# A hybrid encoder on one core: work moved between VectorE, GpSimd and two stages of the kernel, and three loads and adds put elsewhere

## The chip, the cores and the metric

The kernel runs on one core of a Trainium2 chip. The metric is the device time of one execution in microseconds. The profile is one further execution taken by the hardware profiler. Engines are named as the profile names them: PE (TensorE, with PEld for its weight loads), DVE (VectorE), ACT (ScalarE), POOL (GpSimd), and SP, whose queue issues most of the DMAs.

## The reference

An encoder trunk with two layers works on `x` (1024 positions by 1024 channels, float32). Layer 0 mixes positions by attention, layer 1 by a gated MLP over chunks of 128 positions (gMLP); each is followed by a dense MLP with 4096 hidden channels. Every sub-layer has its input normalized and modulated by vectors that come from the condition `c`, and its output gated by one. Cut to what matters here:

```python
for i in range(DEPTH):                       # 2 layers
    mod = silu(c) @ ada_w[i] + ada_b[i]      # six vectors of 1024 for each layer
    sh1, sc1, g1, sh2, sc2, g2 = split(mod, 6)
    h = modulate(rmsnorm(x, norm1_g[i]), sh1, sc1)
    y = gqa_attention(h, ...) if i == 0 else chunked_gmlp(h, ...)
    x = x + g1 * y
    h = modulate(rmsnorm(x, norm2_g[i]), sh2, sc2)
    x = x + g2 * (square(relu(h @ w_in)) @ w_out)

# in gqa_attention: o = softmax(q k^T / 8) v over 16 heads;  return o @ w_o
# in chunked_gmlp:  u, v = split(gelu(h @ w_in + b_in));  v = layernorm(v), mixed within chunks
#                   return (u * v) @ w_out
```

## The kernel before, in words

`x` is held transposed, as 16 tiles of 128 channels by 512 positions: `x[hf][k]`, `hf` the half of the positions and `k` the channel block. Products are made in float32 accuracy from three matmuls of 128x512: each operand is split in a rounded part `hi` (a cast on ACT) and the rest `lo` (a subtraction on DVE); L294 and L295 in `split` do this for activations, L407 and L408 for weights. Large products use one step of a Winograd (Strassen) scheme: seven products of half-size blocks, called "1" to "7", in place of eight. This needs sums of blocks ahead of the matmuls, which are called *forms*, and sums of results behind them. A *unit* below is one product of one pair of blocks: 12 matmuls.

The stages follow one another: q, k and v (0 to 196 us), attention in 64 units (about 190 to 586), the product with `w_o` ("WO", to 674), MLP0's products with `w_in` (to 997, 112 units), MLP0 Out (to 1319, 112 units), gMLP's v (to 1560), gMLP's u (to 1841), gMLP Out (to 2090, 84 units), MLP1's products (to 2406) and MLP1 Out. A table of constants at the end of the file sets when things are done; a scheduler then orders the instructions of each engine, and each engine takes its own in that order. Instructions wrapped in `pin` stay where they are written.

*The vectors from `c`.* Each of the twelve vectors of 1024 is eight columns. Some are made early. `Slabs` makes four groups of eight in attention: a step loads a 128x1024 slab of `ada_w` (L173, on SP, into one of four `w` buffers, three steps ahead), multiplies it on POOL (L186 or L188) and adds it on POOL (L189); at a group's end PE does eight matmuls of one column (L198, tile `am`). A step is taken in 5 of 8 units from unit 10 on. `Halves` makes 24 more columns during MLP0's products, one per step, a step every `MX` = 3 units: two loads of 256 KB (L1214, into two of 16 `x` buffers) and two multiply-sums on DVE (L1226).

*WO's preparation.* At attention's unit `WO_AT` = 53 `load_sel` loads the two halves of a small matrix `sel` (L778, SP) and casts each on DVE (L779); the following units use it in `wo_prep`. The weights of WO come through the same `w` buffers (load L107, cast on ACT L110).

*The heads.* At the start of each MLP and of gMLP the second half's norm is made: squares are summed on DVE (L240), PE sums them over channels (L249, tile `ss`, in unit `HB` = 1 of the MLPs), the root is made, PE spreads it (`rb`, L260), and `forms_b` (from L324) makes the forms of that half: the products with `rb` (`norm_h`, L300), two sums on DVE (L342, L343), a split, and two sums on POOL (L345, L346). For gMLP two of the eight `norm_h` are on POOL (`NB`). Beside them `winograd`'s `prep` makes the weights' sums (L400, L401, L404, L406): on POOL for the first `IG` = 30 units, on DVE after. In `wino_v` (gMLP's v) the sums of block "6" are L1390 to L1392, all on POOL but one.

*The Out stages.* `Out.run` takes the products in the order 1, 2, 6, 4, 7 and then, in a tail, 5 and 3. Results of "6" and "7" that must be added to `x[1]` are kept in tiles and added in the tail's first eight units, `6` at even and `7` at odd units (`add`, L1116: `x<-t` on DVE).

## Time and profile before

| | us |
|---|---|
| median of 3 runs | 2731.7 |
| lowest and highest of these | 2727.88 and 2733.51 |
| the profiled execution | 2724.75 |
| its span on the page | 2723.0 |

The page counts 37313 instructions in the span. PE is busy for 96% of it, DVE 82%, ACT 53%, POOL 39%; the DMA queues move 435 MB. How to read the lines below: a group shows line, engine, operation, the tiles `out<-in` by the program's names, and then busy time or the mean of one in ns; a timeline row shows the start, the duration in us, the engine and the line, and in square brackets how long the engine had idled before it, with what released it; a window shows the length, then for each engine the busy time with the count of instructions, then the granted TensorE clock (1.00 is full), the share of the DMA engines and GB/s.

### The profile page before, as it was taken

Reading aid. Unit: us, or ns where it says so; the run is one execution under the profiler, and the core shown is the slowest. Engines: PE = TensorE matmul, PEld = TensorE weight load, DVE = VectorE, ACT = ScalarE, POOL = GpSimd, SP = SyncE. Lnnn points to the kernel's source line nnn. Section 1 sums busy time; section 2 is a strip of 40 time slices with the busy share of each in tenths; the row PEclk is TensorE's granted clock in tenths of the full one; section 3 lists DMA queues with packets and bytes.
Section 4 is the critical chain, followed back from the end, with each engine's and each line's share of the span. In section 5 each row is a group of like instructions: output and inputs, shape, how many; then the busy total and the mean of one; then the engine's idle time right before and its main releaser. Section 6 shows DMA issues by size and latency. Waiting matters only on the chain. (4 is left out here: it accounts for less than half of the span.)

```text
span 2723.0 us, 37313 instructions
## 1 busy us (share of the span) xinstructions
PE 2627.7 (96%) x12804; PEld 2182.2 (80%) x12804; DVE 2232.0 (82%) x3127; ACT 1450.9 (53%) x2618; POOL 1061.1 (39%) x725
## 2 busy tenths in 40 slices
PE   7999999899899999999999999999999999999999
PEld 5778999787688878877788888887878788878877
DVE  7978888688889889897897767787988887789993
ACT  4559999764654555436443355444446555455432
POOL 1437677644300025451633265556632200035520
PEclk9999999999899999999999999999999999999999
DMA  7120111235386688633334345558641364477461
GB/s 282 62 70 24 50 64 60 80 124 170 97 287 227 217 297 313 211 118 130 114 124 132 114 161 182 182 200 291 223 128 59 128 206 143 166 266 276 143 208 67
DMA packets 207601, 435.39 MB, mean 160 GB/s; under 512 B 22897, under 2 KB 35313, under 8 KB 207410
## 3 DMA queue, kind: packets, MB, share of 16 engines
q1 hardware_dynamic: 180530, 395.24, 43.1%
q10 hardware_dynamic: 26880, 37.76, 3.8%
q8 instruction: 101, 1.65, 0.2%
q14 instruction: 90, 0.74, 0.1%
HBM read 310.23 MB, written 122.68 MB: 159 GB/s over the span
## 5 line engine op out<-in xcount | busy, mean ns | idle before, releaser
L1101 PE MATMUL out<-t,s 128*128 128x512 f32 x1232 | 484.4, 393 | 11.7 <-DVE t L295 11.7
L1102 PE MATMUL out<-t,s 128*128 128x512 f32 x1232 | 482.9, 393 | 7.8 <-DVE s L1085 7.8
L1100 PE MATMUL out<-t,s 128*128 128x512 f32 x1232 | 483.9, 393 | 5.9 <-ACT t L294 5.9
L422 PE MATMUL w<-t,s 128*128 128x512 f32 x1168 | 460.3, 395 | 0.5 <-ACT t L294 0.5
L424 PE MATMUL w<-t,s 128*128 128x512 f32 x1168 | 455.2, 390 | 0.9 <-DVE s L408 0.9
L423 PE MATMUL w<-t,s 128*128 128x512 f32 x1168 | 455.2, 390 | 0.0
L295 DVE TENSOR_TENSOR t<-t,t 128x512 fp32r<-128x512 f32 x408 | 379.6, 944 | 44.7 <-ACT t L294 31.9
L294 ACT CAST t<-t 128x512 fp32r<-128x512 f32 x408 | 244.7, 616 | 174.7 <-DMA t<-hf 57.6
L407 ACT CAST s<-w 128x512 fp32r<-128x512 f32 x292 | 174.7, 618 | 239.2 <-PE w L424 135.2
L1101 PEld LDWEIGHTS out<-t,s 128*128 128x128 f32 x1232 | 233.2, 189 | 66.5 <-DVE t L295 17.4
L1102 PEld LDWEIGHTS out<-t,s 128*128 128x128 f32 x1232 | 233.5, 190 | 59.2 <-DVE s L1085 11.2
L1100 PEld LDWEIGHTS out<-t,s 128*128 128x128 f32 x1232 | 233.1, 189 | 56.9 <-ACT t L294 8.2
L408 DVE TENSOR_TENSOR s<-w,s 128x512 fp32r<-128x512 f32 x292 | 225.0, 778 | 58.9 <-ACT s L407 58.1
L1071 POOL TENSOR_TENSOR w<-w,t 128x512 f32<-128x512 f32 x32 | 50.7, 1590 | 547.8 <-DMA hf<-t 251.7
L422 PEld LDWEIGHTS w<-t,s 128*128 128x128 f32 x1168 | 219.7, 188 | 49.6 <-issue 3.8
L424 PEld LDWEIGHTS w<-t,s 128*128 128x128 f32 x1168 | 219.7, 188 | 47.2 <-DVE s L408 1.3
L423 PEld LDWEIGHTS w<-t,s 128*128 128x128 f32 x1168 | 219.7, 188 | 45.7 <-issue 1.0
L1085 DVE TENSOR_TENSOR s<-t,s 128x512 fp32r<-128x512 f32 x240 | 211.6, 883 | 53.9 <-ACT s L1084 51.8
L1084 ACT CAST s<-t 128x512 fp32r<-128x512 f32 x240 | 147.5, 620 | 169.9 <-PE out L1102 98.4
L878 DVE TENSOR_TENSOR t<-t,t 128x512 fp32r<-128x512 f32 x256 | 164.3, 683 | 23.8 <-ACT t L872 23.4
L855 DVE TENSOR_REDUCE mx<-s 128x1 f32<-128x1024 f32 x128 | 156.5, 1223 | 31.4 <-PE s L852 30.4
L869 PE MATMUL t<-ident,c 128*128 128x128 f32 x1024 | 150.7, 275 | 16.4 <-DVE t L878 11.9
(252 smaller groups left out, 5405.6 us busy)
## 6 DMA issues: line engine op xcount, KB each, us to landing
t<-hf SPq DMA_DIRECT2D x320, 256.0 KB, 3.8
hf<-c SPq DMA_DIRECT2D x156, 256.0 KB, 3.3
w<-in_wi_dram SPq DMA_DIRECT2D x64, 512.0 KB, 4.5
hf<-c ACTq DMA_DIRECT2D x96, 256.0 KB, 2.1
w<-in_adan_dram SPq DMA_DIRECT2D x32, 512.0 KB, 3.3
t<-in_wm_dram SPq DMA_DIRECT2D x64, 256.0 KB, 4.8
wf<-w SPq DMA_DIRECT2D x64, 256.0 KB, 2.9
t<-wf SPq DMA_DIRECT2D x64, 256.0 KB, 3.3
```

Of the source, the lines that this page charges most:

```text
L294: S.copy(hi, src)
L295: (eng or V).tensor_tensor(lo, src, f32(hi), ALU.subtract)
L407: S.copy(hi, src)
L408: V.tensor_tensor(lo, src, f32(hi), ALU.subtract)
L422: T.matmul(ps, hi[:, a], th, start=kt == 0, stop=False)
L423: T.matmul(ps, hi[:, a], tl, start=False, stop=False)
L424: T.matmul(ps, lo[:, a], th, start=False, stop=kt == 3)
L878: pin(V.tensor_tensor(lo, pt, f32(hi), ALU.subtract))
L1085: V.tensor_tensor(lo, src, f32(hi), ALU.subtract)
L1100: T.matmul(ps, hi[:, a], th, start=begin and kt == 0, stop=False)
L1101: T.matmul(ps, hi[:, a], tl, start=False, stop=False)
L1102: T.matmul(ps, lo[:, a], th, start=False, stop=end and kt == 3)
```

## The change

It has six edits. `Slabs` loses the group (1, 2), and these eight columns are made by `Halves`, which now has 32 and takes a step every 2 units. `load_sel` is called at unit 47, and the casts (`copy_sel`, on ACT, pinned) stay at 53. The sums L345 and L346 of `forms_b`, the two `norm_h` of `NB`, and the early sums of `prep` go from POOL to DVE; in `wino_v` the first pair's three sums of "6" go to DVE, and those of the other two pairs stay (one on DVE, two on POOL). `HB` is 2 for MLP0 and stays 1 for MLP1. The adds of the "6" results into `x[1]` start at half of the tail (`tail` is 32 units in the MLPs, 24 in gMLP).

```diff
--- before.py
+++ after.py
@@ -156,7 +156,7 @@
                                1.0, ng[:, layer, which, k : k + 1], ALU.add, ALU.mult)
 
     pending = [(0, j, k) for j in (2, 4, 3) for k in range(KT)]
-    late = [(0, 5, k) for k in range(KT)] + [(1, j, k) for j in (3, 5) for k in range(KT)]
+    late = [(0, 5, k) for k in range(KT)] + [(1, j, k) for j in (2, 3, 5) for k in range(KT)]
 
 
 
@@ -202,7 +202,7 @@
                 V.scalar_tensor_tensor(amod[:, layer, which], mod[:, layer, j], 1.0, ng[:, layer, which],
                                        ALU.add, ALU.mult)
 
-    slabs = Slabs([(1, 1), (1, 0), (1, 2), (1, 4)])
+    slabs = Slabs([(1, 1), (1, 0), (1, 4)])
 
     def mods(n, tag="w"):
         for _ in range(min(n, len(pending))):
@@ -321,7 +321,7 @@
             f["todo"].pop(0)()
             n -= 1
 
-    def forms_b(f, xt, layer, which, rb, order, nb=()):
+    def forms_b(f, xt, layer, which, rb, order):
 
         raw = f.pop("raw")
         src = {q: [None] * 4 for q in "345678"}
@@ -329,8 +329,8 @@
         b12, b22, t3 = src["5"], src["3"], src["7"]
 
         def h(kt):
-            b12[kt] = norm_h(xt[kt], layer, which, kt, rb, G if kt in nb else V)
-            b22[kt] = norm_h(xt[kt + 4], layer, which, kt + 4, rb, G if kt + 4 in nb else V)
+            b12[kt] = norm_h(xt[kt], layer, which, kt, rb, V)
+            b22[kt] = norm_h(xt[kt + 4], layer, which, kt + 4, rb, V)
 
         def forms(kt):
             if kt == 0:
@@ -342,8 +342,8 @@
             V.tensor_tensor(t3[kt], b22[kt], b12[kt], ALU.subtract)
             V.tensor_tensor(t2, b11, t3[kt], ALU.add)
             f[("6", kt)] = split(t2)
-            G.tensor_tensor(b12[kt], b12[kt], b11, ALU.subtract)
-            G.tensor_tensor(b21, b21, t2, ALU.subtract)
+            V.tensor_tensor(b12[kt], b12[kt], b11, ALU.subtract)
+            V.tensor_tensor(b21, b21, t2, ALU.subtract)
 
         def later(q):
             for kt in range(4):
@@ -394,16 +394,15 @@
             hi, lo = w_[:, :512], w_[:, 512:]
             sf[(q, p)] = hi, lo
             src = half(p, {"1": "11", "2": "12", "6": "11", "5": "21", "4": "22", "7": "22", "3": "12"}[q])
-            e = G if i < IG else V
             if q == "6":
                 a11, a21, a22 = (half(p, c) for c in ("11", "21", "22"))
-                e.tensor_tensor(a21, a21, a22, ALU.add)
-                e.tensor_tensor(a11, a21, a11, ALU.subtract)
+                V.tensor_tensor(a21, a21, a22, ALU.add)
+                V.tensor_tensor(a11, a21, a11, ALU.subtract)
             elif q == "4":
                 a12 = half(p, "12")
-                e.tensor_tensor(a12, a12, half(p, "11"), ALU.subtract)
+                V.tensor_tensor(a12, a12, half(p, "11"), ALU.subtract)
             elif q == "7":
-                e.tensor_tensor(src, src, half(p, "11"), ALU.subtract)
+                V.tensor_tensor(src, src, half(p, "11"), ALU.subtract)
             S.copy(hi, src)
             V.tensor_tensor(lo, src, f32(hi), ALU.subtract)
             if q == "3":
@@ -774,10 +773,15 @@
 
     def load_sel():
         for i in range(2):
-            raw, s_ = slot(F32, (32, 512)), slot(F32R, (32, 512))
+            raw = slot(F32, (32, 512))
             nc.sync.dma_start(raw, t["sel"][:, i * 512 : (i + 1) * 512])
-            V.tensor_copy(s_, raw)
-            sel.append(s_)
+            sel.append(raw)
+
+    def copy_sel():
+        for i in range(2):
+            s_ = slot(F32R, (32, 512))
+            pin(S.copy(s_, sel[i]))
+            sel[i] = s_
 
     def wo_sums(hf):
         ri = small.tile([P, 4, NH], F32, tag="ri", name=nm("ri"), bufs=1)
@@ -957,9 +961,11 @@
                 if f == "m":
                     if i in deferred:
                         deferred.pop(i)()
+                    elif i == WO_AT - 6:
+                        load_sel()
                     elif WO_AT <= i < WO_AT + 10:
                         if i == WO_AT:
-                            load_sel()
+                            copy_sel()
                         elif i == WO_AT + 1:
                             wo_sums(0)
                         else:
@@ -1104,8 +1110,11 @@
                     for kt in range(4):
                         del self.f[(b, q, kt)]
                 j = i - self.n + self.tail
-                if 0 <= j < 8:
-                    self.add(1, j % 2, j // 2, self.acc[("67"[j % 2], j // 2)])
+                late = j - self.tail // 2
+                if 0 < j < 8 and j % 2:
+                    self.add(1, 1, j // 2, self.acc[("7", j // 2)])
+                elif 0 <= late < 8 and late % 2 == 0:
+                    self.add(1, 0, late // 2, self.acc[("6", late // 2)])
                 if end:
                     self.take(i, b, q, p, ps, done)
                 if hook:
@@ -1260,7 +1269,7 @@
         def at(i):
             more(f, RW, None)
             if halves:
-                h = i - HB - 12
+                h = i - 13
                 if 0 <= h < 2 * KT:
                     spill(h // KT, (h % KT,))
                 elif h == 2 * KT:
@@ -1271,11 +1280,11 @@
                     halves.load()
                 elif h > 2 * KT + 6 and h % MX == 0:
                     halves.step()
-            if i == HB:
+            if i == HB[layer]:
                 rest.append(norm_ss(sqs[0], bank_y))
-            elif i == HB + 1:
+            elif i == HB[layer] + 1:
                 rest[:] = forms_b(f, x[1], layer, 1, norm_rb(rest[0], bank_y, True), "5473")
-            elif i > HB and rest:
+            elif i > HB[layer] and rest:
                 rest.pop(0)()
             if stores and i % 7 > 0 and i % 7 != 6:
                 stores.pop(0)()
@@ -1387,9 +1396,10 @@
             src = {"1": a11, "2": a12, "7": a11, "5": a21, "4": a22, "3": a12}.get(q)
             if q == "6":
                 src = xslot()
-                G.tensor_tensor(a11, a11, a21, ALU.subtract)
-                (V if p else G).tensor_tensor(src, a22, a11, ALU.subtract)
-                G.tensor_tensor(a12, a12, src, ALU.subtract)
+                e = G if p else V
+                e.tensor_tensor(a11, a11, a21, ALU.subtract)
+                V.tensor_tensor(src, a22, a11, ALU.subtract)
+                e.tensor_tensor(a12, a12, src, ALU.subtract)
             elif q == "5":
                 G.tensor_tensor(a21, a21, a22, ALU.add)
             S.copy(hi, src)
@@ -1501,7 +1511,7 @@
                 spill(0)
                 rest.append(norm_ss(sqB, bank_y))
             elif i == HBV + 2:
-                rest[:] = forms_b(f, x[1], 1, 0, norm_rb(rest[0], bank_y), "7543", NB)
+                rest[:] = forms_b(f, x[1], 1, 0, norm_rb(rest[0], bank_y), "7543")
             elif i > HBV + 2 and rest and (i <= HBV + 6 or i % 2):
                 rest.pop(0)()
                 if len(rest) == 4:
@@ -1647,15 +1657,14 @@
 LO = 3
 TG = ((0, 0), (1, 0), (1, 1), (0, 1))
 CUT = 8
-MX = 3
+MX = 2
 LW = 5
-IG = 30
 SW = 3
 WA = 6
 LW2 = 2
 HK = 3
 LK = 4
-HB = 1
+HB = (2, 1)
 HBV = 1
 PRE = 2
 WO_AT = 53
@@ -1663,7 +1672,6 @@
 RQ = 3
 RW = 2
 NA = (7,)
-NB = (3, 7)
 WOM = (0, 2, 1, 1, 2, 3, 4, 1)
 PREP = ((0, 1, 2), (3, 4, 5), (6, 7))
 QM = (0, 0, 0, 1, 0, 1, 2, 2, 2, 0)
```

On SP, at the end of attention, the loads stood in this order before (`in_adan` are the slabs, `in_sel` the two halves of `sel`, `in_xT` tiles of `x`):

```order
L173 DMA w_5806<-in_adan_dram 128x1024
L173 DMA w_5892<-in_adan_dram 128x1024
L473 DMA x_6939<-in_xT_dram 128x512
L473 DMA x_6941<-in_xT_dram 128x512
L173 DMA w_6060<-in_adan_dram 128x1024
L473 DMA x_6943<-in_xT_dram 128x512
L473 DMA x_6945<-in_xT_dram 128x512
L173 DMA w_6158<-in_adan_dram 128x1024
L778 DMA t_6052<-in_sel_dram 32x512
L173 DMA w_6421<-in_adan_dram 128x1024
L778 DMA t_6056<-in_sel_dram 32x512
```

and now, from behind the last slab on (`in_ada` is a column of the vectors, `in_wo` the first weight of WO):

```order
L777 DMA t_5549<-in_sel_dram 32x512
L777 DMA t_5551<-in_sel_dram 32x512
L472 DMA x_6897<-in_xT_dram 128x512
L472 DMA x_6899<-in_xT_dram 128x512
L472 DMA x_6901<-in_xT_dram 128x512
L472 DMA x_6903<-in_xT_dram 128x512
L472 DMA x_6905<-in_xT_dram 128x512
L472 DMA x_6907<-in_xT_dram 128x512
L472 DMA x_6909<-in_xT_dram 128x512
L472 DMA x_6911<-in_xT_dram 128x512
L139 DMA w_6970<-in_ada_dram 128x1024
L107 DMA w_6975<-in_wo_dram 128x1024
```

Both `sel` loads stand together ahead of the tiles of `x`, and no slab stands behind or between them.

On DVE, at MLP0's head, behind the row that uses `rb` first (`t` are forms, `x` the second half's tiles):

```order
L300 TENSOR_TENSOR t_8092<-x_7117,rb_8070 128x512
L300 TENSOR_TENSOR t_8095<-x_7125,rb_8070 128x512
L300 TENSOR_TENSOR t_8098<-x_7119,rb_8070 128x512
L300 TENSOR_TENSOR t_8101<-x_7127,rb_8070 128x512
L342 TENSOR_TENSOR t_8104<-t_8095,t_8092 128x512
L343 TENSOR_TENSOR t_8105<-t_7641,t_8104 128x512
L295 TENSOR_TENSOR t_8109<-t_8105,t_8108 128x512
L300 TENSOR_TENSOR t_8134<-x_7121,rb_8070 128x512
L300 TENSOR_TENSOR t_8137<-x_7129,rb_8070 128x512
L342 TENSOR_TENSOR t_8140<-t_8101,t_8098 128x512
L343 TENSOR_TENSOR t_8141<-t_7644,t_8140 128x512
L295 TENSOR_TENSOR t_8145<-t_8141,t_8144 128x512
```

and now:

```order
L300 TENSOR_TENSOR t_8070<-x_7075,rb_8048 128x512
L300 TENSOR_TENSOR t_8073<-x_7083,rb_8048 128x512
L300 TENSOR_TENSOR t_8076<-x_7077,rb_8048 128x512
L300 TENSOR_TENSOR t_8079<-x_7085,rb_8048 128x512
L342 TENSOR_TENSOR t_8082<-t_8073,t_8070 128x512
L343 TENSOR_TENSOR t_8083<-t_7599,t_8082 128x512
L345 TENSOR_TENSOR t_8070<-t_8070,t_7599 128x512
L346 TENSOR_TENSOR t_7658<-t_7658,t_8083 128x512
L295 TENSOR_TENSOR t_8087<-t_8083,t_8086 128x512
L295 TENSOR_TENSOR t_8095<-t_7993,t_8094 128x512
L300 TENSOR_TENSOR t_8113<-x_7079,rb_8048 128x512
L300 TENSOR_TENSOR t_8116<-x_7087,rb_8048 128x512
```

L345 and L346, on POOL before, stand behind L343 in each of the four steps, ahead of the split's subtraction L295.

On DVE, in the tail of MLP0 Out (L1085 and L295 are the subtractions that PE's operands wait for; `x<-t` are the adds of kept results, `x<-out` those from PSUM), the scheduler had put the four adds of "6" (`x_11014` to `x_11020`) among the splits:

```order
L295 TENSOR_TENSOR t_12736<-t_12659,t_12735 128x512
L1116 SCALAR_TENSOR_TENSOR x_11016<-t_11103,mod,x_11016 128x512
L295 TENSOR_TENSOR t_12760<-t_12684,t_12759 128x512
L1151 TENSOR_TENSOR t_11163<-out_12694,t_11163 128x512
L1085 TENSOR_TENSOR s_12740<-t_12290,s_12740 128x512
L295 TENSOR_TENSOR t_12784<-t_12709,t_12783 128x512
L1116 SCALAR_TENSOR_TENSOR x_11018<-t_11129,mod,x_11018 128x512
L1116 SCALAR_TENSOR_TENSOR x_10907<-out_12719,mod,x_10907 128x512
L1085 TENSOR_TENSOR s_12764<-t_12320,s_12764 128x512
L295 TENSOR_TENSOR t_12808<-t_12733,t_12807 128x512
L1116 SCALAR_TENSOR_TENSOR x_11020<-t_11163,mod,x_11020 128x512
L1116 SCALAR_TENSOR_TENSOR x_10909<-out_12743,mod,x_10909 128x512
```

The same place now (line numbers are 6 to 9 higher):

```order
L295 TENSOR_TENSOR t_12721<-t_12643,t_12720 128x512
L1091 TENSOR_TENSOR s_12700<-t_12354,s_12700 128x512
L295 TENSOR_TENSOR t_12745<-t_12668,t_12744 128x512
L1160 TENSOR_TENSOR t_11138<-out_12678,t_11138 128x512
L1091 TENSOR_TENSOR s_12725<-t_12383,s_12725 128x512
L295 TENSOR_TENSOR t_12769<-t_12693,t_12768 128x512
L295 TENSOR_TENSOR t_12793<-t_12718,t_12792 128x512
L295 TENSOR_TENSOR t_12817<-t_12742,t_12816 128x512
L1160 TENSOR_TENSOR t_11172<-out_12703,t_11172 128x512
L1091 TENSOR_TENSOR s_12749<-t_12299,s_12749 128x512
L1125 SCALAR_TENSOR_TENSOR x_10916<-out_12728,mod,x_10916 128x512
```

and three of the adds of "6" (`x_11025` to `x_11029` from a `t`) stand here, some 90 rows on; the first, `x_11023`, stands 21 rows ahead of them:

```order
L295 TENSOR_TENSOR t_13369<-t_13302,t_13368 128x512
L1091 TENSOR_TENSOR s_13405<-t_13274,s_13405 128x512
L1091 TENSOR_TENSOR s_13436<-t_13309,s_13436 128x512
L1125 SCALAR_TENSOR_TENSOR x_11025<-t_11112,mod,x_11025 128x512
L295 TENSOR_TENSOR t_13377<-t_13276,t_13376 128x512
L1091 TENSOR_TENSOR s_13461<-t_13337,s_13461 128x512
L1091 TENSOR_TENSOR s_13492<-t_13372,s_13492 128x512
L1125 SCALAR_TENSOR_TENSOR x_11027<-t_11138,mod,x_11027 128x512
L1125 SCALAR_TENSOR_TENSOR x_11029<-t_11172,mod,x_11029 128x512
```

In between are the adds of "7" and the start of the last blocks; the splits that stood around the adds have moved up by one or two rows.

## The prediction

> **What bounds the kernel now.** The page first: the span, and the share of each engine.

> ```profile
> span 2723.0 us, 37313 instructions
> PE 2627.7 (96%) x12804; PEld 2182.2 (80%) x12804; DVE 2232.0 (82%) x3127; ACT 1450.9 (53%) x2618; POOL 1061.1 (39%) x725
> ```

> PE is the bound, so a gain can come only from the 95 us in which it does nothing and from stretches where it runs slowly. The windows view finds those (length, then busy time and instructions of PE, PEld, DVE, ACT, POOL, then the granted clock).

> ```profile
> 480.00:600.00 120.00, 106.13 (x672) 92.10 (x671) 89.10 (x121) 83.72 (x161) 71.04 (x49) 0.94 0.29 94
> 673.00:742.00 69.00, 58.69 (x231) 45.62 (x230) 57.43 (x75) 43.07 (x79) 29.05 (x19) 0.90 0.23 73
> 742.00:1000.00 258.00, 258.00 (x1140) 213.64 (x1139) 222.37 (x412) 131.96 (x225) 5.24 (x4) 1.00 0.76 257
> 1195.00:1250.00 55.00, 50.06 (x212) 39.55 (x211) 49.53 (x63) 23.65 (x45) 20.22 (x13) 0.97 0.48 144
> 1319.00:1370.00 51.00, 43.95 (x182) 33.86 (x181) 47.59 (x56) 26.23 (x44) 38.27 (x26) 0.97 0.15 52
> 1990.00:2045.00 55.00, 49.16 (x200) 38.30 (x199) 48.90 (x63) 22.84 (x43) 18.89 (x12) 0.94 0.44 138
> 2090.00:2152.00 62.00, 57.38 (x237) 45.09 (x235) 50.94 (x72) 42.53 (x77) 23.50 (x15) 0.94 0.21 66
> 2585.00:2640.00 55.00, 51.60 (x219) 41.52 (x218) 51.37 (x67) 20.68 (x38) 19.45 (x13) 0.97 0.53 173
> ```

> 742 to 1000 is full pace: 258/1140 = 0.226 us per matmul. A window's length less its matmuls at that pace is what it loses: 16.7 us at the head of MLP0 (673), 9.8 at that of gMLP (1319), 8.4 at that of MLP1 (2090); 7.0, 9.7 and 5.4 in the three Out tails (1195, 1990, 2585). Every losing window has POOL busy a third of the time or more, the full-pace one hardly at all. These losses are upper bounds, since a few matmul records can be missing. Attention's matmuls differ in shape; its gaps are taken from the timelines below.

> **Part 1: attention (sel, the dropped group).** PE's, then DVE's, SP's and POOL's timelines round the first gap, with the copy that ACT will now make.

> ```profile
> 496.31 0.60 PE L869 MATMUL t<-ident,c 128*128 128x128 f32 x4
> 496.66 0.72 PE L888 MATMUL o<-t,t 128*128 128x256 f32 x4
> 506.46 1.12 PE L869 MATMUL t<-ident,c 128*128 128x128 f32 x4 [9.09 <-DVE t L878]
> 504.26 0.41 DVE L779 CAST t<-t 32x512 fp32r<-32x512 f32 x1 [10.24 <-DMA t<-in_sel_dram]
> 500.76 0.34 SPq L173 DMA_DIRECT2D w<-in_adan_dram  x1
> 501.21 0.37 SPq L778 DMA_DIRECT2D t<-in_sel_dram  x1
> 498.40 2.34 POOL L189 TENSOR_TENSOR s<-s,w 128x1024 f32<-128x1024 f32 x1
> 509.99 0.57 ACT L792 CAST t<-rt 32x512 fp32r<-32x512 f32 x1
> ```

> The small second sel load stood on SP behind an adan load, which waited for a w buffer until POOL's sum ended at 500.74. DVE stood 10.24 us at the cast, and behind it the copy L878 that PE needed: 9.09 us. Now the loads go out six units earlier, on SP behind the last adan load and ahead of the x loads, and ACT makes the casts when they have long landed: −9.1. The four transposes behind the gap took 1.12 against 0.60 ahead of it, about half pace. The next gap, 37 us on, shows both groups behind it.

> ```profile
> 535.81 2.40 POOL L189 TENSOR_TENSOR s<-s,w 128x1024 f32<-128x1024 f32 x1
> 538.24 0.33 SPq L107 DMA_DIRECT2D w<-in_wo_dram  x1
> 541.56 1.04 ACT L110 CAST s<-w 128x1024 fp32r<-128x1024 f32 x1 [3.96 <-DMA w<-in_wo_dram]
> 543.63 1.11 PE L869 MATMUL t<-ident,c 128*128 128x128 f32 x4 [4.02 <-ACT t L841]
> 544.40 1.20 PE L888 MATMUL o<-t,t 128*128 128x256 f32 x4
> 566.38 1.95 PE L198 MATMUL am<-ones,s 128*128 128x1 f32 x16
> ```

> The first wo load, too, waited for a slab's buffer (POOL done at 538.21, load at 538.24), ACT stood 3.96 us at its cast, and PE 4.02 us behind ACT. With one group gone the w buffers are free by then: −4.0. The two groups behind it took 1.11 + 1.20 = 2.31 us against 0.60 + 0.72 = 1.32; the slow stretch runs a little past them, so 1.0 each is the least: −1.2 for the first gap, −1.3 for the second. Two ACT casts of 0.57 at unit 53 come back, about half of them hidden behind PE: +0.5. A group's end is eight small matmuls on PE, 16 in the profile as L249's four are 8: one end fewer is −1.9. Sum: −9.1 − 1.2 + 0.5 − 4.0 − 1.3 − 1.9 = **−17.0**. Ends: −12, if the wo cast, some 20 ACT rows earlier now, still meets its load late by 4 us and takes that back with what follows it; −20, if the slow stretches cost twice those 1.2 and 1.3 and ACT's casts nothing.

> **Part 2: POOL's sums to DVE at three heads.** Timelines of DVE, POOL and PE there.

> ```profile
> 678.30 1.78 DVE L240 TENSOR_TENSOR t<-t,t 128x512 f32<-128x512 f32 x1
> 677.91 1.62 POOL L401 TENSOR_TENSOR w<-w,w 128x512 f32<-128x512 f32 x1 [1.94 <-issue]
> 685.35 1.87 PE L249 MATMUL ss<-ones,t 128*128 128x1 f32 x8 [4.95 <-DVE t L240]
> 697.08 1.74 POOL L345 TENSOR_TENSOR t<-t,t 128x512 f32<-128x512 f32 x1 [4.07 <-DVE t L342]
> 718.78 4.37 DVE L295 TENSOR_TENSOR t<-t,t 128x512 fp32r<-128x512 f32 x3
> 2131.53 1.88 DVE L295 TENSOR_TENSOR t<-t,t 128x512 fp32r<-128x512 f32 x3
> ```

> A DVE sum of two SBUF tiles lasts 1.78 us when a POOL sum starts beside it; three in a row take 1.88 alone and 4.37 beside POOL. So alone it costs about 0.60, and a POOL sum can hold one back by 1.1: moved, each costs 0.60 and returns up to 1.1. DVE's busy time less 0.60 per instruction bounds the waits in a window: 12.4 us at MLP0 (57.43 − 75 × 0.60), 7.7 at MLP1, 14.0 at gMLP.
> - MLP0: 18 sums move, 10.8 us of new DVE work against 12.4 back. About six of the waits lie ahead of ss, 6.6 us against seven moved sums at 4.2: ss comes 2.4 earlier. HB puts one more unit, 12 × 0.226 = 2.7 us, on PE ahead of it. Together that covers the 4.95 us stall: **−5**. POOL's share of the ss chain (the power for rstd) also no longer stands behind sums. Behind rb I count nothing. Ends: −12 (most of the window's 16.7) and +2 (rb, a unit later, makes the forms late).
> - MLP1: 11 sums, 6.6 against 7.7 back; 1.1, doubled since the matmuls behind a gap ran at half pace: **−2** (−5 to +1).
> - gMLP: 18 sums, 10.8 against at most 14.0, of which part stays, as the sums of q5 and of q6's second and third pair stay on POOL: **0** (−3 to +3).

> [...]

> **Part 3: four adds moved in each Out tail.** In the MLP0 tail, DVE and then PE:

> ```profile
> 1199.70 1.78 DVE L1116 SCALAR_TENSOR_TENSOR x<-t,mod,x 128x512 f32<-128x512 f32 x1
> 1213.50 0.74 DVE L1116 SCALAR_TENSOR_TENSOR x<-t,mod,x 128x512 f32<-128x512 f32 x1
> 1228.08 0.50 PE L1100 MATMUL out<-t,s 128*128 128x512 f32 x1 [1.62 <-ACT t L294]
> 1229.62 0.79 PE L1101 MATMUL out<-t,s 128*128 128x512 f32 x1 [1.04 <-DVE t L295]
> 1230.63 0.63 PE L1100 MATMUL out<-t,s 128*128 128x512 f32 x1
> 1231.06 0.63 PE L1101 MATMUL out<-t,s 128*128 128x512 f32 x1
> ```

> and the window that follows, where the order now has the adds:

> ```profile
> 1250.00:1280.00 30.00, 30.00 (x134) 24.75 (x133) 24.89 (x39) 19.15 (x33) 1.30 (x1) 1.00 0.11 36
> ```

> DVE is 90% busy there (49.53 of 55) and its casts L295 reach PE late. Four adds of about 0.66 leave: 2.6 us, or 6.8 if each were held as at 1199.70. They now stand eight units or more later, where DVE has 5 us of 30 free and PE loses nothing. After the gaps matmuls start 0.43 us apart (1230.63, 1231.06) against 0.226, which I count as 0.9: **−3.5** here and at gMLP Out, where the loss is larger; **−1** at MLP1, where it is 5.4 and begins ahead of these adds. Sum −8, ends 0 and −14. [...]

> **Part 4: eight more vectors in MLP0's products.** The group of multiply-sums, its accumulator reads, and a window within.

> ```profile
> L1226 DVE SCALAR_TENSOR_TENSOR x<-x,x x48: 679/684/691, 798.8 to 986.8; 128x512 f32<-128x512 f32 x48
> L1226 DVE DVE_READ_ACCUMULATOR x<-x,x x48: 80/82/85, 799.4 to 987.4; 128x1 f32 x48
> 810.00:990.00 180.00, 180.00 (x796) 149.05 (x795) 159.90 (x309) 91.58 (x156) 0.00 (x0) 1.00 0.68 232
> ```

> A vector is two of these pairs, 2 × (0.60 + 0.08) = 1.4 us. Steps come every second unit (5.4 us) instead of every third (8.1): in 180 us 33 instead of 22, so DVE goes from 159.90 to about 175, 97%. PE is not held as long as it stays under 100%: **+1**. Ends: 0, and +12, if only a third of its 20 idle us can be filled (15 − 7 = 8 over, and half as much again in slow matmuls). The 16 more loads of 256 KB lie on SP, at a DMA share of 0.68.

> **Sum.** −17.0 − 5 − 2 + 0 − 8 + 1 = −31. The profiled execution took 2724.75 us, 1.75 over its span and 7 under the median; it goes to 2693.8, and the median from 2731.7 to **2701**. A measurement can tell about 0.2%, 5.5 us, from no change.

> **The rivals.**
> - *Attention alone.* DVE does its waiting as work, and the heads and tails come out even. For it: 10.8 against 12.4 is close. Against: ss gets a spare unit, and the adds truly leave a full engine. −17 + 1: 2716.
> - *More than counted.* Half of what the six windows lose goes (57.0/2 = 28.5), with attention at −20 and the products at 0: −48.5, 2683. For it: POOL stands in all of them. Against: DVE remains 85% busy or more there.
> - *It does not do what it says.* sel or wo lands late all the same, and DVE's load takes the rest: 2730. Against: no adan load stands ahead of them with a POOL sum still to come.
> - *Slower, by the SP queue.* In MLP0's products the vector loads wait on SP for x buffers, as sel did behind adan, and the wi loads behind them come late. With 16 x buffers, two for the condition vector and three pairs in flight, eight are left for spilled tiles. From the point where these run out, ten pairs held by half of what sel was, 4.6 us each, are +46 against the −32 of the other terms: 2746. Against: at 0.68 DMA share PE lost nothing there. A DVE over 100% instead would be the +12 above, not enough to turn the sign.

> **How the numbers follow.** My forecast has 0.65, attention alone 0.18, more 0.09, no change 0.04, slower 0.04. Attention alone and more bound the range: 2681 and, with 3 us for an unlucky wo cast, 2719. Past them lie the 0.08 of the last two, a third of the 'more' case and about 0.05 of the forecast's and attention's own bad ends, 0.16 in all. Faster by over 0.2%: 0.65 + 0.18 + 0.09 less 0.01 for bad ends = 0.91; same 0.05 (no change, and those 0.01); slower 0.04.

> **What would show it.** Right: no gap over 2 us on PE before units 53 to 60; clock near 1.00 in the attention's end; no DVE sum near 1.78 at the MLP heads; the ss matmul with under 2 us of wait; the MLP0 tail's loss about halved; DVE near 97% in the products, with PE still at 0.226 per matmul. Wrong: a wait of DVE on sel; DVE busier and PE no less idle at the heads (attention alone); PE waiting for s<-w casts or wi loads between 800 and 1000 us (slower).

## The result, and the profile after

The changed kernel takes 2683.6 us (median of 4 runs, 2680.66 to 2685.52) against 2730.15 before: a ratio of 0.9828, 95% interval 0.9811 to 0.9845, or 46.6 us less. The forecast was 2701, 31 less; the direction and the range (2681 to 2719) held, with the result near its lower end, and the gain is half as large again as the sum. The profiled execution fell from 2724.75 to 2680.66 us. First the page's totals, then the windows that answer to those of before.

```profile
span 2678.8 us, 37196 instructions
PE 2610.3 (97%) x12788; PEld 2169.8 (81%) x12788; DVE 2246.6 (84%) x3242; ACT 1446.2 (54%) x2620; POOL 897.5 (34%) x626
```

```profile
469.22:590.00 120.78, 118.11 (x761) 101.86 (x761) 102.43 (x138) 95.63 (x182) 40.73 (x39) 1.00 0.27 93
655.70:724.00 68.30, 63.43 (x271) 49.07 (x270) 62.60 (x104) 46.45 (x84) 1.01 (x1) 1.00 0.29 100
770.00:942.00 172.00, 172.00 (x761) 142.41 (x760) 159.58 (x329) 79.75 (x141) 0.00 (x0) 1.00 0.73 260
1161.00:1216.00 55.00, 52.63 (x232) 42.41 (x231) 49.92 (x61) 26.48 (x50) 22.98 (x15) 1.00 0.44 147
1285.00:1336.00 51.00, 43.19 (x176) 33.70 (x175) 45.52 (x74) 25.92 (x44) 7.45 (x5) 0.90 0.14 48
1953.00:2008.00 55.00, 52.66 (x232) 42.45 (x231) 50.67 (x64) 27.90 (x52) 21.88 (x14) 1.00 0.41 133
2053.40:2115.00 61.60, 59.78 (x262) 47.80 (x260) 56.42 (x95) 43.39 (x78) 1.01 (x1) 1.00 0.25 90
2541.00:2596.00 55.00, 52.32 (x224) 42.81 (x223) 49.91 (x65) 21.07 (x39) 19.97 (x13) 0.97 0.48 168
```

By the same reckoning (length less matmuls at 0.2263 us) the heads now lose 7.0 us at MLP0 (655), 11.2 at gMLP (1285) and 2.3 at MLP1 (2053); the tails 2.5, 2.5 and 4.3. That is 29.8 for 57.0 before. Two things stand out. At MLP1's head DVE is *busier* than before (56.42 us against 50.94) and PE loses 6.1 us less. And the clock: 0.90, 0.94, 0.97 and 0.94 before are 1.00 now at the MLP heads and the first two tails, but at gMLP's head it fell from 0.97 to 0.90.

Each stage can be measured from its first matmul to the next stage's first (the last stage to its last matmul). In us against before, in the profiled executions of all the single edits too, and in a second profiled execution of the changed kernel (the run changed_again, further down):

| | attention, WO | MLP0 products | MLP0 Out | gMLP v, u | gMLP Out | MLP1 products | MLP1 Out |
|---|---|---|---|---|---|---|---|
| the changed kernel | −17.9 | −9.9 | −6.4 | +1.1 | −3.7 | −6.2 | −1.3 |
| the changed kernel again | −16.5 | −8.2 | −6.5 | +0.9 | −3.4 | −6.2 | −0.3 |
| sel_only | −10.6 | +1.8 | −0.2 | +1.5 | −1.7 | −0.3 | +1.2 |
| group_only | −14.7 | +1.1 | −0.6 | +1.5 | +0.7 | +2.6 | +0.8 |
| heads_only | +0.7 | −9.8 | −0.9 | +1.0 | +2.7 | −6.2 | +1.6 |
| adds_only | −0.7 | +0.8 | −6.6 | −0.1 | −5.1 | +1.4 | −0.6 |

Stages that an edit leaves alone move by up to 2.7 us from one execution to the next; much of it is at an Out stage's head, where gMLP Out's unit 9 lost 5.2 us before, 7.4 now, and 2.6 to 8.3 in the other runs. So one entry tells 3 us or more. group_only's profiled execution is also the slowest of its four (2715.8 us against 2708.6 to 2711.0), so its row understates that edit.

The two executions of the changed kernel differ by 1.7 us in MLP0's products, and the clock says why. In both PE waits 2.90 us for `rb`. Here are two stretches of 3.41 us round that wait, laid so that the falls of the clock begin at their borders; the second execution stands first:

```profile
669.21:672.62 3.41, 0.51 (x3) 0.20 (x2) 0.76 (x2) 1.53 (x5) 1.01 (x1) 1.00 0.00 0
672.62:676.03 3.41, 3.41 (x7) 2.00 (x7) 1.66 (x3) 1.15 (x3) 0.00 (x0) 0.50 0.00 0
```

```profile
666.48:669.89 3.41, 1.64 (x8) 1.02 (x6) 2.06 (x5) 0.79 (x3) 1.01 (x1) 1.00 0.00 0
669.89:673.30 3.41, 2.28 (x8) 1.58 (x9) 1.12 (x2) 1.94 (x6) 0.00 (x0) 1.00 0.00 0
```

In the one, the whole wait fell into one stretch (2.90 us idle), and the next 3.41 us ran at a clock of 0.50, which by that figure costs half of them, 1.7 us (an estimate); in the other it was divided between two stretches (1.77 and 1.13 us idle), and the clock stayed at 1.00. So the 1.00 at MLP0's head, and 1.7 of its 9.9 us, are luck; the clocks and gains at MLP1's head and in the first two tails came out alike in both.

### The profile page after: what moved, and what is told of

It reads as the page before. It is cut to its first block, busy times and chain, and to the rows that moved or that the text cites. A ratio compares the mean times of both kernels' runs of the same rounds, so it can differ in the third digit from the quotient of the medians.

```text
span 2678.8 us, 37196 instructions
## 1 busy us (share of the span) xinstructions
PE 2610.3 (97%) x12788; PEld 2169.8 (81%) x12788; DVE 2246.6 (84%) x3242; ACT 1446.2 (54%) x2620; POOL 897.5 (34%) x626
## 5 line engine op out<-in xcount | busy, mean ns | idle before, releaser
L295 DVE TENSOR_TENSOR t<-t,t 128x512 fp32r<-128x512 f32 x408 | 356.6, 887 | 42.5 <-ACT t L294 25.2
L294 ACT CAST t<-t 128x512 fp32r<-128x512 f32 x408 | 243.8, 616 | 166.9 <-DVE t L295 59.9
L1107 PEld LDWEIGHTS out<-t,s 128*128 128x128 f32 x1232 | 232.6, 189 | 64.0 <-DVE t L295 15.3
L1091 DVE TENSOR_TENSOR s<-t,s 128x512 fp32r<-128x512 f32 x240 | 212.5, 888 | 49.6 <-ACT s L1090 48.5
L882 DVE TENSOR_TENSOR t<-t,t 128x512 fp32r<-128x512 f32 x256 | 164.4, 683 | 21.6 <-ACT t L876 21.2
L859 DVE TENSOR_REDUCE mx<-s 128x1 f32<-128x1024 f32 x128 | 156.6, 1223 | 29.6 <-PE s L856 28.5
L892 PE MATMUL o<-t,t 128*128 128x256 f32 x1024 | 162.6, 291 | 0.0
```

The source lines that it names most:

```text
L294: S.copy(hi, src)
L295: (eng or V).tensor_tensor(lo, src, f32(hi), ALU.subtract)
L882: pin(V.tensor_tensor(lo, pt, f32(hi), ALU.subtract))
L1091: V.tensor_tensor(lo, src, f32(hi), ALU.subtract)
L1107: T.matmul(ps, hi[:, a], tl, start=False, stop=False)
```

## The experiments

**1. Each edit alone, on the kernel before.** Four runs on one chip, beside 2729.2 us for the kernel before (15 runs). sel_only moves the loads of `sel` and makes its casts on ACT, and nothing else:

```diff
+                    elif i == WO_AT - 6:
+                        load_sel()
...
-                            load_sel()
+                            copy_sel()
```

> The kernel before with one edit: sel loaded at unit 47, its casts on ACT at unit 53. Theory (each attention term comes from its own edit): the 9.1 us gap and the slow matmuls behind it go, two short ACT casts come back, about -9.8 against before; the wo gap of 4.0 us and the third and fourth slab ends stay. Rival (the dropped group gives all of it, because the load only waited behind slabs that are gone then): the same -9.8 here, but then the group alone gives as much (see group_only). Second rival (the next wait takes its place: w buffers hold sel's neighbours back in any case): under -3.

Measured 2717.1 us, ratio 0.9962 (0.9947 to 0.9976), −12.1. group_only moves the eight columns:

```diff
+    late = [(0, 5, k) for k in range(KT)] + [(1, j, k) for j in (2, 3, 5) for k in range(KT)]
+    slabs = Slabs([(1, 1), (1, 0), (1, 4)])
+MX = 2
```

> The kernel before with one edit: the group (1, 2) made in MLP0's products, a step every 2 units; sel still loaded at unit 53 and cast on DVE. Theory (each term by its own edit): the wo gap with its slow matmuls (5.3) and one slab end (1.9) go, the products cost 0 to 1: about -7, and DVE still stands for sel. Rival (the early load is not needed once the slabs end by unit 48): sel finds SP free and only its own landing of some 2 us is left, so about -14 to -16.

Measured 2710.1 us, ratio 0.9938 (0.9924 to 0.9953), −19.0: as much as sel_only and more, 16.5 us by the first matmul of WO. Its SP and DVE timelines say why: with the slabs used up, no slab's load holds up sel's. Both go out at 482.97, 18 us before the time at which the second went before (501.21), and DVE's casts do not wait.

```profile
479.98 1.76 SPq L473 DMA_DIRECT2D x<-in_xT_dram  x4
482.97 1.72 SPq L778 DMA_DIRECT2D t<-in_sel_dram  x2
```

```profile
494.63 0.74 DVE L779 CAST t<-t 32x512 fp32r<-32x512 f32 x2
```

So the rival holds: the two edits are two cures for one wait. The second gap goes with the group alone (4.02 us before, 1.33 in group_only). sel_only keeps it, on ACT and on PE behind:

```profile
530.40 1.04 ACT L110 CAST s<-w 128x1024 fp32r<-128x1024 f32 x1 [4.07 <-DMA w<-in_wo_dram]
```

```profile
532.47 1.11 PE L874 MATMUL t<-ident,c 128*128 128x128 f32 x4 [4.15 <-ACT t L846]
```

heads_only makes the sums of the heads on DVE, with `HB` 1 for both MLPs (in part; the lines of `norm_h`, `prep` and `wino_v` are as in the change):

```diff
-            G.tensor_tensor(b12[kt], b12[kt], b11, ALU.subtract)
-            G.tensor_tensor(b21, b21, t2, ALU.subtract)
+            V.tensor_tensor(b12[kt], b12[kt], b11, ALU.subtract)
+            V.tensor_tensor(b21, b21, t2, ALU.subtract)
...
-            e = G if i < IG else V
```

> The kernel before with the sums of the three heads on DVE, HB still 1. The changed kernel lost 9.9 us less in MLP0's products, 6.2 less in MLP1's, and 1.2 more in gMLP v. Theory A (each moved sum returns more than it costs and PE keeps its full clock; HB does little): -13 to -16. Theory B (HB brought MLP0's half, as the prediction had it): -8 to -11. [...]

Measured 2714.4 us, ratio 0.9951 (0.9936 to 0.9966), −14.8. Theory A: MLP0's products gain 9.8 us and MLP1's 6.2, all that the changed kernel has there. Its PE at MLP0's head, and its DVE (the stage starts at 674.3, before at 673.6):

```profile
682.76 1.07 PE L249 MATMUL ss<-ones,t 128*128 128x1 f32 x8 [2.89 <-DVE t L240]
688.10 1.02 PE L260 MATMUL rb<-t,ones 128*128 128x512 f32 x2
```

```profile
677.75 0.68 DVE L240 TENSOR_TENSOR t<-t,t 128x512 f32<-128x512 f32 x1
678.36 0.68 DVE L403 TENSOR_TENSOR w<-w 128x512 f32<-128x512 f32 x1
678.96 0.68 DVE L400 TENSOR_TENSOR w<-w,w 128x512 f32<-128x512 f32 x1
679.56 0.68 DVE L295 TENSOR_TENSOR t<-t,t 128x512 fp32r<-128x512 f32 x1
```

and PE's row for `rb` before:

```profile
692.34 1.48 PE L260 MATMUL rb<-t,ones 128*128 128x512 f32 x2
```

Of DVE's rows from 672 to 690 us no TENSOR_TENSOR lasts over 0.69 us, and POOL has no sum of 128x512 from 670 to 702. Before, the L240 at 678.30 stood beside POOL's L401 (677.91 to 679.53): it lasted 1.78 us and ended 0.55 us behind it. This holding back is what two expectations below call the exclusion. From the stage's start, ss comes at 8.5 us for 11.75 before, and rb at 13.8 for 18.7; the ss matmuls (eight in the profile) take 1.07 for 1.87.

adds_only starts the adds of "6" at half of the tail:

```diff
+                late = j - self.tail // 2
+                if 0 < j < 8 and j % 2:
+                    self.add(1, 1, j // 2, self.acc[("7", j // 2)])
+                elif 0 <= late < 8 and late % 2 == 0:
+                    self.add(1, 0, late // 2, self.acc[("6", late // 2)])
```

> The kernel before with the adds of the 6 results started at half of the tail. The changed kernel's tails lost 4.5, 3.7 and 1.3 us less by units. Theory (the adds alone do it): -8 to -10, with MLP0's tail loss down from 9.5 to 5. Rival (the tails gained from something else that moved, such as the order that the scheduler found): under -4.

Measured 2716.4 us (ten runs, 2710.0 to 2724.9), ratio 0.9960 (0.9948 to 0.9972), −12.8; in the profiled execution the three Out stages make 12.3. That is the theory, and somewhat more than its 8 to 10. Its window at the MLP0 tail shows the same clock of 1.00 as the changed kernel, and 4.1 us lost for 7.0 before:

```profile
1194.00:1249.00 55.00, 51.39 (x225) 41.01 (x224) 49.88 (x65) 26.91 (x51) 20.18 (x13) 1.00 0.47 147
```

**2. Which sums, and is HB worth anything?** Runs on the changed kernel, again on one chip.

```diff
-HB = (2, 1)
+HB = (1, 1)
```

> The changed kernel with HB 1 for both MLPs. The heads alone, at HB 1, gained 9.8 us in MLP0's products. Theory (HB is worth nothing once the sums are off POOL): within 2 us of the changed kernel, about 2684, and the head of MLP0 loses about 7 us as now. Rival (the prediction's: the spare unit covers half of the ss wait): 3 to 5 us slower, about 2688.

Measured 2685.4 us (2684.61 to 2686.51); MLP0's products 1.3 us longer than in the changed kernel's first execution and 0.4 shorter than in its second. HB does next to nothing. In the changed kernel ss no longer waits, but rb does:

```profile
664.22 1.05 PE L249 MATMUL ss<-ones,t 128*128 128x1 f32 x8
671.02 1.12 PE L260 MATMUL rb<-t,ones 128*128 128x512 f32 x2 [2.90 <-ACT t L255]
```

The 2.89 us ahead of ss in heads_only became 2.90 ahead of rb. DVE's order shows why. It must take the result of ss (L251) before the root can be made; first in the changed kernel, then in hb_back:

```profile
668.41 0.15 DVE L251 TENSOR_SCALAR ms<-ss 128x4 f32<-128x4 f32 x1
```

```profile
667.72 0.15 DVE L251 TENSOR_SCALAR ms<-ss 128x4 f32<-128x4 f32 x1
```

With HB 2, PE is done with ss at 665.27 and DVE comes to L251 3.1 us later, behind sums and subtractions that its order has ahead of it; with HB 1, PE is done at 667.31 and DVE 0.4 us later. From the stage's start L251 stands at 12.7 us with HB 2 and 10.8 with HB 1, so rb comes no earlier with HB 2 (15.3 us for 15.1). PE has spent the unit in front, and the wait is only in another place.

forms_back puts L345 and L346 back on POOL, prep_back the weights' sums of the first 30 units:

```diff
-            V.tensor_tensor(b12[kt], b12[kt], b11, ALU.subtract)
-            V.tensor_tensor(b21, b21, t2, ALU.subtract)
+            G.tensor_tensor(b12[kt], b12[kt], b11, ALU.subtract)
+            G.tensor_tensor(b21, b21, t2, ALU.subtract)
```

> The changed kernel with L345 and L346 (the two form sums) on POOL again at all three heads, the weights' sums still on DVE. Theory (what counts are POOL's sums beside DVE's, wherever they stand; forms are 8 of MLP0's 18 and 8 of MLP1's 11): MLP0 gives back 3 to 5 of its 9.9, MLP1 4 to 5 of its 6.2, gMLP gains 1 to 3: 5 to 8 slower than the changed kernel, about 2690. Rival (only sums ahead of the ss matmul count, since that wait is the large one): no more than 2 slower in the MLPs.

```diff
+            e = G if i < IG else V
...
-                V.tensor_tensor(src, src, half(p, "11"), ALU.subtract)
+                e.tensor_tensor(src, src, half(p, "11"), ALU.subtract)
```

> The changed kernel with the weights' sums of the first 30 units on POOL again (MLP0, MLP1 and gMLP u), the forms' sums on DVE. Theory (each POOL sum counts): MLP0 gives back 4 to 6 of its 9.9, MLP1 1 to 2 of its 6.2: 5 to 8 slower than the changed kernel. Rival (the forms' sums make the loss, being waited for behind rb): within 2 of it.

forms_back took 2688.4 us (2687.13 to 2689.84), 4.8 over the changed kernel: MLP0's products +2.6, MLP1's +4.5, gMLP −0.9, against its first execution. prep_back took 2691.8 (2691.34 to 2692.01), 8.2 over: MLP0's +7.1, MLP1's 0.0. In MLP0 the two add up to 9.7, near its whole gain of 9.9 (against the second execution, 6.3 of 8.2); the weights' sums are nearly three quarters of it or more there and nothing in MLP1, where the forms make the gain. MLP1's head in both, forms_back first:

```profile
2054.70:2116.30 61.60, 58.09 (x242) 46.11 (x241) 50.47 (x79) 42.68 (x77) 13.85 (x9) 0.94 0.18 62
```

```profile
2063.10:2124.70 61.60, 59.92 (x262) 47.70 (x261) 56.43 (x89) 43.63 (x79) 10.85 (x8) 1.00 0.25 89
```

POOL works about as long in the one as in the other (13.85 and 10.85 us), but only the forms' sums cost PE anything, 20 matmuls and six hundredths of the clock. The theory that each POOL sum counts alike falls; what counts is what it stands beside.

sums_out leaves them out on every engine:

```diff
-            V.tensor_tensor(b12[kt], b12[kt], b11, ALU.subtract)
-            V.tensor_tensor(b21, b21, t2, ALU.subtract)
...
+            if i < IG:
+                pass
```

> The changed kernel with the moved sums left out at the heads of the MLPs and of gMLP u, on any engine: L345, L346 and the weights' sums of the first 30 units (the forms 4 and 5 and the weights' blocks 4, 6 and 7 are then not what they should be). It shows what the 0.60 us each still costs on DVE. Theory A (DVE is the bound of the heads, so its work counts): MLP0's head, that now loses 7.0 us in 655.7 to 724, loses 3 or less, MLP1's 2.3 goes below 1, gMLP gains 3 to 5. Theory B (the gain was the clock and the exclusion, and the work now hides): under 1.5 us in each head.

One run, 2670.45 us: MLP0's products 5.3 us shorter than in the changed kernel's first execution (7.0 than in its second), gMLP 3.8, MLP1's 0.9. Theory A for MLP0 and gMLP: DVE still sets their pace, and MLP0's 18 sums of 0.60 (10.8 us) cost PE half of that or more. In MLP1 the work hides.

**3. Can it be better?** `defer` makes the two form sums just ahead of the splits that use them:

```diff
-            V.tensor_tensor(b12[kt], b12[kt], b11, ALU.subtract)
-            V.tensor_tensor(b21, b21, t2, ALU.subtract)
+            wait[kt] = b11, b21, t2
...
             for kt in range(4):
+                b11, b21, t2 = wait[kt]
+                if q == "5":
+                    V.tensor_tensor(b12[kt], b12[kt], b11, ALU.subtract)
+                elif q == "4":
+                    V.tensor_tensor(b21, b21, t2, ALU.subtract)
                 f[(q, kt)] = split(src[q][kt])
```

> The changed kernel with L345 and L346 still on DVE, but made only ahead of the splits that use them (forms 5 and 4) instead of ahead of the split of form 6. Leaving the moved sums out bounds what can be had: 5.3 us in MLP0's products, 3.8 in gMLP, 0.9 in MLP1's. Theory (at the heads DVE's order is what PE waits for; a sum is free once it stands where DVE has idle time): 4 to 8 less than the changed kernel, about 2678. Rival (DVE's total work in the head counts, whatever its order): within 2 of it.

defer_gmlp also gives gMLP's first three sums of "6" back to POOL (the lines of `wino_v` as before), and defer_hb3 is defer with one number changed:

```diff
-HB = (2, 1)
+HB = (3, 1)
```

> As defer, with the three sums of gMLP's block 6 of the first pair on POOL again, which then has hardly anything else to do there. Theory (in gMLP DVE itself is the bound from 1295 to 1330, so work taken off it returns more than the exclusion costs): 2 to 4 us less than defer in gMLP v. Rival (each POOL sum holds a DVE sum back by more than it saves): 2 to 5 more than defer.

> As defer, with HB 3 for MLP0: the ss matmul one more unit later. HB 1 to 2 was worth 1.3 us. Theory (the ss wait was covered by the sums, and rb's wait of 2.9 us only moves behind another unit): within 1.5 of defer. Rival (the later ss makes the forms late): 2 or more slower.

> The changed kernel as it is, on the chip of the three others, to compare them with: 2681 to 2686.

On one chip the changed kernel (changed_again) took 2684.1 us (2681.89 to 2685.24), defer 2680.5 (2678.98 to 2681.97), defer_gmlp 2678.2 (2676.21 to 2684.99) and defer_hb3 2677.5 (2675.34 to 2679.28). Against before the last is 0.9811 (0.9794 to 0.9827), the changed kernel there 0.9834 (0.9818 to 0.9851). These intervals overlap; the runs of the two themselves do not.

The stages here are compared with changed_again. In gMLP, defer is 2.6 us shorter, so order counts there; in MLP0 it changed nothing (+0.1), and there its theory falls: the whole gain of 3.6 us is short of its 4 to 8. defer_gmlp's gMLP is 4.3 shorter, 1.7 better than defer's: with the sums off DVE, at a clock of 0.97 for 0.93, though POOL works 24.70 us for 9.25. That is the theory's sign and a size too small to be sure of (the profiled execution is also the slowest of its five). defer_hb3's MLP0 is 3.4 us shorter, against both expectations: the ss and the rb wait are both gone there, while defer still waits 2.89 us for rb. rb itself comes hardly earlier (15.0 us from the stage's start for 15.3), but PE now has a unit to do meanwhile, and the 3.41 us at half clock that follow the wait in defer are gone (the clock of this window is 1.00 for 0.98). Its MLP0 head loses 5.2 us. PE's rows of defer, then of defer_hb3, and the latter's window:

```profile
672.73 1.97 PE L260 MATMUL rb<-t,ones 128*128 128x512 f32 x2 [2.89 <-ACT t L255]
```

```profile
668.62 0.95 PE L249 MATMUL ss<-ones,t 128*128 128x1 f32 x8
672.42 1.13 PE L260 MATMUL rb<-t,ones 128*128 128x512 f32 x2
```

```profile
657.40:725.70 68.30, 65.90 (x279) 50.39 (x278) 63.97 (x107) 46.73 (x85) 1.01 (x1) 1.00 0.33 111
```

HB 3 without the deferred sums was not run, so whether it needs them stays open.

## Why the prediction was right, and where its sizes were off

**Attention: −17.0, measured −17.9 (−16.5 in the second execution).** The sum was right, the shares were not: the sum holds because the change has both edits, and says nothing of what each is worth. The 9.1 of sel did not need the early load: without the fourth group no adan load is left to stand ahead of it. The early load alone brings 10.6 to 11.2, the group 14.7 to 16.5, both 17.9 to 18.6. The casts of sel and the wo cast, now early, wait little (0 and 1.47 us on ACT), and the largest gap that PE has between 485 and 560 us is 1.07:

```profile
492.97 1.14 ACT L783 CAST t<-t 32x512 fp32r<-32x512 f32 x2
510.64 1.05 ACT L110 CAST s<-w 128x1024 fp32r<-128x1024 f32 x1 [1.47 <-DMA w<-in_wo_dram]
```

```profile
513.33 0.99 PE L873 MATMUL t<-ident,c 128*128 128x128 f32 x7 [1.07 <-ACT c L865]
```

**MLP0's head: −5, measured −9.9 (−8.2).** This is a term that was mis-sized, in two of its steps. "HB puts one more unit on PE" was to cover half of the stall; alone, hb_back has it at 1.3 us or nothing. "Behind rb I count nothing": units 9 to 18 lost 7.4 us before and 3.0 in heads_only. The first half was nearly right (ss 3.3 earlier, 2.4 forecast), but rb came 4.9 earlier, and with the shorter stalls slow matmuls went too. Before, PE idled 10.3 us of the 16.7 that the window lost, so 6.4 were slow pace; now it idled 4.9 of 7.0, and 2.1 were.

**MLP1's head: −2, measured −6.2.** I set the waits that DVE would lose, 7.7 us, against the work that it would get, 6.6, doubled the difference and took it for PE's gain. The 6.6 was a miscount as well: of POOL's 15 instructions in that window 14 are sums (8 of the forms, 6 of the weights) and one makes the root, not 11, so the same reckoning would have been 8.4 against 7.7, a small loss. DVE's busy time did rise. What PE waited for were single operations in the order of ACT and DVE, some of them held up beside a POOL sum. Before, DVE's sum L343 and the subtraction L295 behind it were held (one of the POOL sums is that at 2116.19), and later three L295 in a row took 4.54 us beside POOL's sums of the weights:

```profile
2114.62 1.49 DVE L343 TENSOR_TENSOR t<-t,t 128x512 f32<-128x512 f32 x1
2117.23 1.15 DVE L295 TENSOR_TENSOR t<-t,t 128x512 fp32r<-128x512 f32 x1
2125.26 4.54 DVE L295 TENSOR_TENSOR t<-t,t 128x512 fp32r<-128x512 f32 x3
```

```profile
2116.19 1.65 POOL L346 TENSOR_TENSOR t<-t,t 128x512 f32<-128x512 f32 x1 [0.63 <-DVE t L343]
```

PE's two long waits there end with ACT's cast L294 and with DVE's L295:

```profile
2118.37 0.50 PE L422 MATMUL w<-t,t 128*128 128x512 f32 x1 [1.73 <-ACT t L294]
2132.26 0.50 PE L424 MATMUL w<-t,t 128*128 128x512 f32 x1 [2.10 <-DVE t L295]
```

That the held sums made both waits is argued from these rows, not shown row by row; that moving the forms' sums removes the loss is shown by forms_back. Idle time fell from 4.6 to 1.8 us, and slow pace from 3.8 to 0.5.

**gMLP's head: 0, measured +1.1**, inside what runs differ by (sel_only and group_only, which leave it alone, have +1.5). It is where the rival "attention alone" holds: DVE is nearly full there (93% before, 89% now), and work given to it costs about what the exclusion did.

**The tails: −8, measured −11.4 by stages.** In the MLP0 tail PE's idle time fell from 4.94 to 2.37, about the four adds of 0.66; the pace gave 1.9 more, where I had 0.9. Before, the clock was at half for 3.41 us from 1229.14 on; PE had worked for 1.22 of the 3.41 us ahead of that, and no gap of it in this tail was over 1.62:

```profile
1225.73:1229.14 3.41, 1.22 (x3) 0.48 (x3) 3.41 (x5) 2.18 (x4) 1.27 (x1) 1.00 0.07 22
1229.14:1232.55 3.41, 2.94 (x7) 2.35 (x8) 3.41 (x5) 1.15 (x2) 1.52 (x1) 0.50 0.75 231
```

So PE idled for 2.19 us of the stretch ahead of the fall. What is left in this tail now is one gap of 1.12 us and one of 1.05, and the clock is 1.00:

```profile
1182.55 0.50 PE L1108 MATMUL out<-t,s 128*128 128x512 f32 x1 [1.12 <-DVE s L1091]
1197.07 0.50 PE L1107 MATMUL out<-t,s 128*128 128x512 f32 x1 [1.05 <-DVE t L295]
```

**The products: +1, measured 0.** While the vectors are made (770 to 942 us) DVE is busy for 159.58 us of 172, 93% and not 97%, and PE runs 761 matmuls at 0.226 us without a gap, so neither DVE nor a late load held it and the slower rival has nothing for it.

Of the rivals, "more than counted" was nearest: 27.2 of 57.0 us lost in the six windows went, close to its half.

## What to carry to other kernels

Price a moved operation by the wait that it stands ahead of, in its engine's order, and not by the sum of an engine's busy time: at MLP1's head DVE got busier (56.42 us for 50.94) and PE waited less (1.8 us for 4.6). A stall of TensorE cost about one and a half times its length here or more (16.7 us lost for 10.3 idle, 8.4 for 4.6), where the granted clock fell behind it (0.90 and 0.94 in these windows); and as the same stall of 2.90 us met a fall in one execution and none in another, one profile is not enough to tell 2 us. Where two edits remove the same wait, say what each is worth alone, or the sum of their terms has no test.
